# Head norms of a diffusion-transformer projection: the reciprocal root refined with one operand of every step in PSUM

## The chip, the core and the metric

The program runs on one core of one Trainium2 chip, as one launch. The metric is the device time of one execution in microseconds (us). The core has five engines that each work through their own queue in order: TensorE (PE in the profile; PEld is its loading of weights), VectorE (DVE), ScalarE (ACT), GpSimd (POOL) and SyncE (SP, which issues the DMAs here). They wait for one another through semaphores. On-chip data lies in SBUF, and in PSUM, into which TensorE writes its products.

## The reference, cut to what matters

Two layers of a hybrid backbone run over 128 context tokens and 1024 latent tokens of width 1024. Each layer projects the normalised tokens to a convolution input, to queries, keys and values of a grouped-query attention (GQA) and to those of a neighbourhood attention; after the mixing there is an output projection and an MLP. The change touches only the normalisation of the query and key heads, 64 wide:

```python
def _rms(x, g):
    xf = x.astype(jnp.float32)
    y = xf * lax.rsqrt(jnp.mean(xf * xf, axis=-1, keepdims=True) + EPS)
    return (y * g.astype(jnp.float32)).astype(x.dtype)
...
    qa = _rms(qa.reshape(B, L, GQA_HEADS, HEAD_DIM), aqg)
    ka = _rms(ka.reshape(B, L, GQA_KV_HEADS, HEAD_DIM), akg)
...
    qn = _rms(qn.reshape(B, L, NA_HEADS, HEAD_DIM), nqg)
    kn = _rms(kn.reshape(B, L, NA_HEADS, HEAD_DIM), nkg)
```

## The kernel before

Matrix products are done in float32 from split operands (high and low parts, three products each). The program is written out in a fixed order by nested Python generators; every engine executes its instructions in just that order, and the tile framework adds the semaphores. SBUF tiles come from tagged pools (T with 18 buffers, S with 18, U with 19, V with 24), PSUM tiles from one pool of eight banks (`P`, line 87): a new tile waits until the earlier user of its buffer is done.

The stage around the change is the projection (`project`, from line 689). Seven column blocks (A0 to A5 and VN, 256 columns each) are run over the nine token tiles in five groups, four of two tiles and one of a single tile. One such group does, in this order:

- `tok_group` (lines 534 to 544): 24 matmuls per token tile on TensorE into a PSUM bank `pst` (lines 541 to 543).
- In groups 1 and 3, `pr.step()`: the weights of the next column block are split, the high part `wh` on ScalarE (line 96) and the low part `wl` on VectorE (line 99), and further weights are requested.
- The first half of `post` (line 492): `head_stats` squares the heads on ScalarE (`sq`), sums them on VectorE (`ss`, line 420), and `rsq_start` takes Ln and Exp(-0.5 x) on ScalarE, which gives a first value `y` of the reciprocal root.
- A step of the convolution (`conv_taps`, line 572): the 31 taps of channel half 0 run on VectorE (`cacc<-cin,vecs,cacc`, 1167 wide), one or two in a step; 22 taps of half 1 run as a product on ScalarE (`cp`) and an addition on GpSimd (`cacc<-cacc,cp`, line 570).
- The second half of `post`: `head_norm` refines `y` by one Newton step, three scalar_tensor_tensor instructions on VectorE (`rsq_end`, lines 167 to 171, all recorded at line 102), each [128, 2 to 8] in size, and multiplies the heads by it (`xn<-pst,y`, line 99). GpSimd then applies gains (line 471) or rotary tables (lines 484 to 490) to `xn` and writes `o`.
- In groups 0, 2 and 4, a step of `fill`, the modulation for later in the layer (`modulation`, line 183): eight of its steps multiply into a bank `psmod` (line 224) with weights `aw` by DMA; then VectorE copies it (`mt<-psmod`, line 229), and at the next step TensorE transposes it (`psmt<-ident,mt`, line 233).
- `flush`: SyncE stores `o` of two groups before to DRAM (`ddA<-o`). From block A5 on the GQA's preparation (`kd<-ddA`, transposes at line 784) is interleaved.

`rsq_start` and `rsq_end` are shared with the row norms (lines 280, 282) and the convolution's layer norm (lines 744, 746), which the change leaves alone.

Of the kernel before, what the change touches and what calls it, by code (L numbers as in the profile page):

```python
# [14 lines left out]
ACTF = mybir.ActivationFunctionType  # L15
ALU = mybir.AluOpType
# [9 lines left out]
DH = 64  # L26
EPS = 1e-6
# [18 lines left out]
def hybrid_step(ctx, tc, I, O, depth=DEPTH):  # L46
# [7 lines left out]
    def nm(p):  # L54
        count[0] += 1
        return f"{p}{count[0]}"
# [4 lines left out]
    def T(shape, dt=F32, n="t"):  # L61
        return pers.tile([128] + list(shape), dt, tag="T", bufs=N_T, name=nm(n))
# [4 lines left out]
    def V(shape, n="v"):  # L67
        return pers.tile([128] + list(shape), F32, tag="V", bufs=24, name=nm(n))
# [18 lines left out]
    def P(n="ps"):  # L87
        return psum.tile([128, 512], F32, tag="p", bufs=8, name=nm(n))
# [3 lines left out]
    def act(out, in_, func, scale=1.0, bias=0.0, **k):  # L92
        nc.scalar.activation(out=out, in_=in_, func=func, scale=scale, bias=bias, **k)  # L93
# [4 lines left out]
    def tt(out, a, b, op, eng=None):  # L98
        (eng or nc.vector).tensor_tensor(out=out, in0=a, in1=b, op=op)  # L99

    def stt(out, a, s, b, op0, op1):
        nc.vector.scalar_tensor_tensor(out=out, in0=a, scalar=s, in1=b, op0=op0, op1=op1)  # L102
# [7 lines left out]
    eps = pers.tile([128, 1], F32, name="eps")  # L110
# [51 lines left out]
    def rsq_start(q, y, m):  # L162

        act(y, q, ACTF.Ln, scale=1.0 / m, bias=eps)
        act(y, y, ACTF.Exp, scale=-0.5)

    def rsq_end(q, y, t, m):

        stt(t, y, -0.5 / m, y, ALU.mult, ALU.mult)
        stt(t, q, EPS * m, t, ALU.add, ALU.mult)  # L170
        stt(y, t, 1.5, y, ALU.add, ALU.mult)
# [239 lines left out]
    def heads4(a, nt):  # L411

        return a.rearrange("p t (h d) -> p t h d", d=64)

    def head_stats(x, nt):
        n = nt * (x.shape[2] // 64)
        sq = T([nt, x.shape[2]], n="sq")
        act(sq, x, ACTF.Square)
        ss = V([n], "ss")
        nc.vector.tensor_reduce(out=ss, in_=sq.rearrange("p t (h d) -> p (t h) d", d=64), op=ALU.add, axis=AX.X)  # L420
        y = V([n], "y")
        rsq_start(ss, y, DH)
        return x, nt, n, ss, y

    def head_norm(x, nt, n, ss, y):
        rsq_end(ss, y, V([n], "nt"), DH)
        w = x.shape[2]
        xn = T([nt, w], n="xn")
        tt(heads4(xn, nt), heads4(x, nt), y.rearrange("p (t h) -> p t h", t=nt).unsqueeze(3).to_broadcast([128, nt, w // 64, 64]), ALU.mult)
        return xn  # L430
# [61 lines left out]
    def post(L, c, t, nt, ps):  # L492
# [5 lines left out]
        if normed is not None:  # L498
            st = head_stats(x[:, :, normed], nt)
# [4 lines left out]
        if normed is not None:  # L504
            xn = head_norm(*st)
            if c in ("A0", "A1"):
                post_rope(L, c, t, nt, xn, o)
            else:
                gain(o[:, :, normed], xn, 2 if c in ("A2", "A3") else 3, nt, L)
# [1473 lines left out]
```

## Time and profile before

| what | value |
|---|---|
| median of 3 runs | 2981.17 us (2978.42 to 2985.02) |
| the profiled execution | 2982.7 us, of which the span 2980.9 us |
| busy share of the span | PE 95%, PEld 85%, DVE 70%, ACT 47%, POOL 22% |
| mean granted TensorE clock | 0.983 of full |
| where the projections lie | about 100 to 350 us and 1590 to 1830 us |

The profile is one execution, recorded by the chip's profiler. Rows that group instructions name the line, the engine, the operation, the tiles written and read, the shapes and the count, then the busy time and the mean duration of one, and the engine's idle time before them with what ended it. An instruction's duration runs from its start on the engine to its end, so a wait inside the engine (for a memory port, say) lies in the duration, while a wait for a semaphore lies in the idle time before it. Many helpers record at one line (102 for every scalar_tensor_tensor), so groups are told apart by their tiles.

### The profile page before, as it was taken

To read this page: it belongs to the slowest core of one execution; us is meant where nothing else is said; L and a number is where in the kernel's file an instruction comes from. 1 tells how busy PE (TensorE), PEld (TensorE's weight loads), DVE (VectorE), ACT (ScalarE), POOL (GpSimd) and SP (SyncE) were. 2 spreads that over 40 slices of the span, in tenths; PEclk is the share of its full clock that TensorE was granted. 3 is DMA by queue.
4 is the path that set the end of the run, shared out by engine and by line. 5 is a ranking of instruction groups with operands and counts; after the bars stand their busy time and mean duration, and the time that the engine had idled before them with its cause. 6 is when DMAs were issued, how large, how long until landed. Compare 5 with 4: busy or idle time off the path is not lost.

```text
span 2980.9 us, 52857 instructions
## 1 busy us (share of the span) xinstructions
PE 2844.0 (95%) x20328; PEld 2525.2 (85%) x20328; DVE 2096.1 (70%) x4009; ACT 1401.0 (47%) x2864; POOL 652.5 (22%) x607
## 2 busy tenths in 40 slices
PE   6998999999999999999889989999999999999999
PEld 3878745789999989999868886458999999999999
DVE  6588778764867756768675877788557677585676
ACT  4333356762744443433452353668537444433343
POOL 3576345420000000000224772463100000000000
PEclk8999999999999999999999999999999999999999
DMA  7276302424466678443333672024245666565334
GB/s 286 85 210 167 106 20 61 102 65 139 148 212 198 208 239 300 161 156 96 122 129 106 187 200 75 16 55 111 89 124 179 207 203 196 201 236 183 116 102 161
DMA packets 434876, 444.05 MB, mean 149 GB/s; under 512 B 120512, under 2 KB 308672, under 8 KB 434624
## 3 DMA queue, kind: packets, MB, share of 16 engines
q1 hardware_dynamic: 434624, 440.67, 47.4%
q8 instruction: 160, 2.62, 0.4%
q14 instruction: 92, 0.75, 0.1%
HBM read 307.41 MB, written 133.17 MB: 148 GB/s over the span
## 4 chain that ended last, share of the span: by engine, by line
PE 76%; DVE 13%; ACT 4%; issue 2%; DMA 2%; POOL 2%; SPq 1%; DVEq 0%; POOLq 0%; ACTq 0%
PE ps L1319 23%; PE psb L1319 8%; PE psc L1319 6%; PE pso L1319 5%; PE psa L1319 5%; PE psd L1319 3%; PE psacc L1118 3%; PE pspv L985 2%; DVE cacc L102 2%; PE pspt L969 2%; PE pst L541 2%; PE pst L542 2%; PE pst L543 2%; PE psst L1132 2%; PE psm L1044 2%
## 5 line engine op out<-in xcount | busy, mean ns | idle before, releaser
L1319 PE MATMUL ps<-ts,w2h 128*128 128x288 f32 x3072 | 534.4, 296 | 8.3 <-DVE ts L99 4.8
L1319 PEld LDWEIGHTS ps<-ts,w2h 128*128 128x128 f32 x3072 | 451.7, 189 | 9.3 <-DVE ts L99 5.3
L1319 PE MATMUL ps<-ts,w2l 128*128 128x288 f32 x1536 | 329.2, 295 | 0.1
L96 ACT CAST ts<-ti 128x576 fp32r<-128x576 f32 x256 | 172.1, 672 | 310.2 <-PE ps L1319 208.6
L541 PE MATMUL pst<-wh,HA 128*128 128x256 f32 x1040 | 297.9, 286 | 0.0
L542 PE MATMUL pst<-wl,HA 128*128 128x256 f32 x1040 | 294.3, 283 | 0.2 <-DVE wl L99 0.2
L543 PE MATMUL pst<-wh,HA 128*128 128x256 f32 x1040 | 293.7, 282 | 0.0
L93 ACT ACTIVATE ev<-ev 128x576 f32<-128x576 f32 x240 | 164.7, 686 | 265.1 <-DVE ev L99 261.3
L1319 PEld LDWEIGHTS ps<-ts,w2l 128*128 128x128 f32 x1536 | 247.6, 189 | 0.4 <-DVE w2l L99 0.3
L102 DVE SCALAR_TENSOR_TENSOR X<-ps,mod,X 128x288 f32<-128x288 f32 x336 | 112.2, 410 | 163.5 <-PE ps L1319 163.5
L99 DVE TENSOR_TENSOR ts<-ti,ts 128x576 fp32r<-128x576 f32 x256 | 195.5, 764 | 44.7 <-ACT ts L96 44.7
L541 PEld LDWEIGHTS pst<-wh,HA 128*128 128x128 f32 x1040 | 198.3, 191 | 19.2 <-issue 6.9
L542 PEld LDWEIGHTS pst<-wl,HA 128*128 128x128 f32 x1040 | 198.2, 191 | 0.5 <-DVE wl L99 0.4
L543 PEld LDWEIGHTS pst<-wh,HA 128*128 128x128 f32 x1040 | 198.2, 191 | 0.0
L99 POOL TENSOR_TENSOR nacc<-nacc,nsq 128x512 f32<-128x512 f32 (+1 forms) x12 | 15.8, 1320 | 822.2 <-PE ps L1319 796.3
L1772 POOL COPY yu<-X 128x128 f32<-128x128 f32 x8 | 3.9, 500 | 836.2 <-DVE X L102 824.3
L1319 PE MATMUL pso<-HA,woh 128*128 128x288 f32 x1024 | 177.8, 295 | 0.0
L1046 DVE TENSOR_REDUCE mx<-psm 128x1 f32<-128x384 f32 x288 | 142.3, 547 | 30.1 <-PE psm L1044 30.0
L93 ACT ACTIVATE pt<-psst 128x512 f32<-128x512 f32 x216 | 118.1, 597 | 89.6 <-PE psst L1133 88.7
L99 POOL TENSOR_TENSOR R<-R,pt 128x1024 f32<-128x1024 f32 x60 | 148.3, 2472 | 26.3 <-ACT pt L93 24.3
L1319 PEld LDWEIGHTS pso<-HA,woh 128*128 128x128 f32 x1024 | 149.7, 188 | 0.0
L102 DVE SCALAR_TENSOR_TENSOR cacc<-cin,vecs,cacc 128x1167 f32<-128x1167 f32 x78 | 136.8, 1754 | 11.3 <-POOL cacc L570 10.1
(279 smaller groups left out, 7222.6 us busy)
## 6 DMA issues: line engine op xcount, KB each, us to landing
ti<-hd SPq DMA_DIRECT2D x128, 576.0 KB, 4.0
hd<-ev SPq DMA_DIRECT2D x224, 288.0 KB, 4.2
w1r<-in_mlp_w SPq DMA_DIRECT2D x176, 256.0 KB, 4.0
aw<-in_ada_w SPq DMA_DIRECT2D x160, 256.0 KB, 4.0
HF<-in_mlp_w SPq DMA_DIRECT2D x128, 256.0 KB, 5.3
ddA<-o SPq DMA_DIRECT2D x144, 128.0 KB, 3.0
wr<-in_w_in SPq DMA_DIRECT2D x28, 512.0 KB, 4.1
sd<-ev SPq DMA_DIRECT2D x24, 576.0 KB, 2.8
```

The source lines that it names most:

```text
L93: nc.scalar.activation(out=out, in_=in_, func=func, scale=scale, bias=bias, **k)
L96: nc.scalar.copy(out, in_)
L99: (eng or nc.vector).tensor_tensor(out=out, in0=a, in1=b, op=op)
L102: nc.vector.scalar_tensor_tensor(out=out, in0=a, scalar=s, in1=b, op0=op0, op1=op1)
L541: mm(o, hi, wh, start=(k == 0), stop=False)
L542: mm(o, hi, wl, start=False, stop=False)
L543: mm(o, lo, wh, start=False, stop=(k == KT - 1))
L969: nc.tensor.transpose(ps[0:n, c], self.p[j][:, o:o + n], ident)
L985: mm(ps[64 * j:64 * j + 64, 0:128], v[j], self.at[j, i], start=(i == 0), stop=(i == nb - 1))
L1046: nc.vector.tensor_reduce(out=mx[j][:, qt, b:b + 1], in_=ps[:, 0:384], op=ALU.max, axis=AX.X)
L1118: mm(acc[64 * j:64 * j + 64, :], v, pt[:, j, :], start=(kt == 0), stop=(kt == 8))
L1319: mm(ps[h][:, 0:HH], x, y[:, h * HH:(h + 1) * HH], start=(start and z == 0), stop=(stop and z == 2), skip_group_check=True)
```

## The change

`head_stats` no longer calls `rsq_start`. It takes a PSUM bank `pss`, in which two small areas z and t lie, and ScalarE writes the first value twice: once as z in PSUM, once as y in SBUF. `head_norm` does the same Newton step as before, y * (1.5 - 0.5 * (ss/64 + eps) * y * y), with z and t in PSUM: in each of the three instructions one tensor operand is in PSUM and the other in SBUF, where before both were in SBUF. The number of VectorE instructions stays; ScalarE has one Exp more in each of the 60 head norms, and 60 more tiles are taken from the eight PSUM banks.

```diff
         y = V([n], "y")
-        rsq_start(ss, y, DH)
-        return x, nt, n, ss, y
-
-    def head_norm(x, nt, n, ss, y):
-        rsq_end(ss, y, V([n], "nt"), DH)
+        small = P("pss")
+        z, t = small[:, 0:n], small[:, 64:64 + n]
+        act(y, ss, ACTF.Ln, scale=1.0 / DH, bias=eps)
+        act(z, y, ACTF.Exp, scale=-0.5)
+        act(y, y, ACTF.Exp, scale=-0.5)
+        return x, nt, n, ss, y, z, t
+
+    def head_norm(x, nt, n, ss, y, z, t):
+
+        stt(t, y, -0.5 / DH, z, ALU.mult, ALU.mult)
+        stt(z, ss, EPS * DH, t, ALU.add, ALU.mult)
+        stt(y, z, 1.5, y, ALU.add, ALU.mult)
         w = x.shape[2]
```

## The prediction

> **What bounds the kernel now.** I read the page first, then the busy times by stretch, then TensorE's waits in the two stretches where head norms run, and last the order of instructions around the longest of these waits.
>
> ```profile
> span 2980.9 us, 52857 instructions
> PE 2844.0 (95%) x20328; PEld 2525.2 (85%) x20328; DVE 2096.1 (70%) x4009; ACT 1401.0 (47%) x2864; POOL 652.5 (22%) x607
> ```
> ```profile
> 100.00:350.00 250.00, 233.01 (x1798) 207.42 (x1797) 182.36 (x249) 84.87 (x171) 148.46 (x118) 0.97 0.59 163
> 190.00:257.00 67.00, 61.28 (x500) 58.12 (x499) 60.18 (x66) 22.94 (x44) 42.02 (x21) 0.95 0.62 163
> ```
>
> In the second fence the columns after the length are the busy time of PE, PEld, DVE, ACT and POOL, then the granted TensorE clock. TensorE sets the time: in the projection of the first layer it is busy 233 of 250 us, so a change to VectorE can only win what lies in the 17 us where TensorE stands, plus what the stops do to its clock. VectorE is at its limit only locally: 60.2 of 67 us between 190 and 257.
>
> TensorE's own waits in the first layer's stretch, and the matching one of the second layer (us in total, times, longest):
>
> ```profile
> PE psmod L224 <- DMA aw<-in_ada_w: 5.9, 5, 1.7
> PE psmt L233 <- DVE mt L229: 5.7, 1, 5.7
> PE pstr L784 <- DMA kd<-ddA: 3.1, 1, 3.1
> ```
> ```profile
> PE psmt L233 <- DVE mt L229: 5.5, 1, 5.5
> PE pstr L784 <- DMA kd<-ddA: 2.4, 1, 2.4
> ```
>
> The one that VectorE causes is `mt`, the copy of the modulation's product: 5.7 + 5.5 = 11.2 us. The copy itself is short; it comes late because VectorE's queue is late:
>
> ```profile
> 241.43 0.69 DVE L99 TENSOR_TENSOR xn<-pst,y 128x512 f32<-128x512 f32 x1
> 242.04 0.68 DVE L229 COPY mt<-psmod 128x512 f32<-128x512 f32 x1
> ```
> ```profile
> 242.87 1.09 PE L233 MATMUL psmt<-ident,mt 128*128 128x128 f32 x4 [5.72 <-DVE mt L229]
> ...
> 244.40 0.41 PE L541 MATMUL pst<-wh,HA 128*128 128x256 f32 x1
> 244.61 0.41 PE L542 MATMUL pst<-wl,HA 128*128 128x256 f32 x1
> ...
> 247.60 0.28 PE L543 MATMUL pst<-wh,HA 128*128 128x256 f32 x1
> 247.72 0.28 PE L541 MATMUL pst<-wh,HA 128*128 128x256 f32 x1
> ```
>
> TensorE had nothing from 237.15 (242.87 less 5.72). After the stop its matmuls start every 0.21 us, three us later every 0.12: the stop also costs clock.
>
> **The change part by part.** The three steps of the root write and read [128, 2 to 8]. Over both layers, minimum, median and maximum in ns, with the multiplication behind them for comparison:
>
> ```profile
> L102 DVE SCALAR_TENSOR_TENSOR nt<-y x60: 147/223/2679, 120.4 to 1785.5; 128x8 f32<-128x8 f32 x32, 128x4 f32<-128x4 f32 x24, 128x2 f32<-128x2 f32 x4
> L102 DVE SCALAR_TENSOR_TENSOR y<-nt,y x60: 161/168/2645, 120.8 to 1787.4; 128x8 f32<-128x8 f32 x32, 128x4 f32<-128x4 f32 x24, 128x2 f32<-128x2 f32 x4
> L99 DVE TENSOR_TENSOR xn<-pst,y x60: 291/691/693, 121.0 to 1790.2; 128x512 f32<-128x512 f32 x32, 128x256 f32<-128x256 f32 x24, 128x128 f32<-128x128 f32 x4
> ```
> ```profile
> 194.95 2.89 DVE L102 SCALAR_TENSOR_TENSOR cacc<-cin,vecs,cacc 128x1167 f32<-128x1167 f32 x2
> 197.76 2.66 DVE L102 SCALAR_TENSOR_TENSOR nt<-y 128x4 f32<-128x4 f32 x1
> 200.45 0.16 DVE L102 SCALAR_TENSOR_TENSOR nt<-ss,nt 128x4 f32<-128x4 f32 x1
> ```
> ```profile
> 197.18 3.22 POOL L570 TENSOR_TENSOR cacc<-cacc,cp 128x1167 f32<-128x1167 f32 x1 [3.49 <-ACT cp L93]
> ...
> 203.85 2.71 POOL L570 TENSOR_TENSOR cacc<-cacc,cp 128x1167 f32<-128x1167 f32 x1 [1.66 <-ACT cp L93]
> ```
>
> A step with four elements per partition takes 2.66 us when GpSimd's addition runs (197.18 + 3.22 = 200.40; the step ends at 200.42), and 0.16 us otherwise. So a VectorE instruction with two SBUF inputs stands until GpSimd's instruction is over. `xn`, with one input in PSUM, sits right behind the steps and in 60 cases never exceeds 0.693 us. That is the evidence that the new form does not stand. What the steps cost in all:
>
> ```profile
> L102 DVE SCALAR_TENSOR_TENSOR nt<-y 128x8 f32<-128x8 f32 (+2 forms) x60 | 41.7, 696 | 13.3 <-ACT y L93 13.3
> L102 DVE SCALAR_TENSOR_TENSOR y<-nt,y 128x8 f32<-128x8 f32 (+2 forms) x60 | 32.1, 535 | 2.1
> L102 DVE SCALAR_TENSOR_TENSOR nt<-ss,nt 128x8 f32<-128x8 f32 (+2 forms) x60 | 22.1, 368 | 2.1
> ```
>
> 41.7 + 32.1 + 22.1 = 95.9 us for 180 steps; at 0.165 us each, about their undisturbed duration, they need 29.7. So 66 us of standing goes, 33 in each layer. Most is off the path: where VectorE keeps up with TensorE it then only waits longer for the next squares.
>
> How much of the 5.7 us stop goes depends on the queue between 190 and 257, where VectorE's backlog forms. Removed standing can come back in VectorE's other instructions with two SBUF inputs, the taps and `wl`, because they share the same port with GpSimd. I therefore add up what the port must carry there:
>
> ```profile
> L570 POOL TENSOR_TENSOR cacc<-cacc,cp 128x1167 f32<-128x1167 f32 x10 | 30.2, 3019 | 16.2 <-ACT cp L93 16.2
> L471 POOL TENSOR_TENSOR o<-xn,gains 128x512 f32<-128x512 f32 x4 | 7.2, 1801 | 5.0 <-DVE xn L99 5.0
> L471 POOL TENSOR_TENSOR o<-xn,gains 128x256 f32<-128x256 f32 x5 | 4.7, 933 | 3.2 <-DVE xn L99 3.2
> ```
> ```profile
> L102 DVE SCALAR_TENSOR_TENSOR cacc<-cin,vecs,cacc 128x1167 f32<-128x1167 f32 x14 | 26.8, 1916 | 0.2
> L102 DVE SCALAR_TENSOR_TENSOR nt<-y 128x4 f32<-128x4 f32 x4 | 8.1, 2031 | 0.0
> L99 DVE TENSOR_TENSOR wl<-wr,wh 128x1024 fp32r<-128x1024 f32 x3 | 6.1, 2033 | 0.2 <-ACT wh L96 0.2
> ```
>
> GpSimd: 10 x 2.71 = 27.1 us of additions, and at most 7.2 + 4.7 = 11.9 of gains. VectorE: 14 taps at 2.89/2 = 1.45, 20.2 us; three `wl`, an estimate of 1.3 each from the tap's time and their 1024 to 1167 elements, 3.8. Together 63.0 of 67 us; the 27 steps add 27 x 0.165 = 4.5 and fill the stretch entirely (67.5). So the port is full before, and the change takes about 4.5 us of its load away, and with it the pairs of instructions that waited on each other. As the gains' rows still hold GpSimd's own standing, 11.9 is an upper end and the slack rather 6 to 7 us. I take 5 us less backlog at `mt` in each layer. That leaves a stop of 0.7 and 0.5 us, and a gain of 10 us over both layers.
>
> The clock in a stretch with short stops of TensorE (at most 1.7 us each, the `psmod` row), and behind the two stops for `mt`:
>
> ```profile
> 145.00:150.00 5.00, 2.17 (x9) 0.47 (x7) 4.71 (x7) 0.60 (x1) 4.92 (x6) 1.00 0.90 264
> ```
> ```profile
> 243.00:246.00 3.00, 3.00 (x15) 3.00 (x16) 3.00 (x3) 0.78 (x3) 0.47 (x1) 0.50 0.53 112
> 1723.00:1727.00 4.00, 4.00 (x28) 4.00 (x27) 3.84 (x8) 1.94 (x4) 0.67 (x1) 0.75 0.61 131
> ```
>
> Half a clock over 3 us is 1.5 us, a quarter less over 4 us is 1.0. Short stops leave the clock at 1.00 (2.17 of 5 us busy in the first row), so residues under 1 us should too: 2.5 us gained. [...]
>
> What the change adds:
>
> ```profile
> L99 DVE TENSOR_TENSOR mod<-psmt,vecs x12: 157/165/175, 44.8 to 1835.4; 128x16 f32<-128x16 f32 x12
> L93 ACT ACTIVATE y<-y x60: 203/208/211, 117.5 to 1785.2; 128x8 f32<-128x8 f32 x32, 128x4 f32<-128x4 f32 x24, 128x2 f32<-128x2 f32 x4
> L102 DVE SCALAR_TENSOR_TENSOR nt<-psn,nt x14: 224/691/692, 40.9 to 2248.0; 128x512 f32<-128x512 f32 x8, 128x64 f32<-128x64 f32 x4, 128x128 f32<-128x128 f32 x2
> ```
>
> A small VectorE instruction with an input in PSUM takes 0.165 us, as the steps do now: 0 for the new operand. The other end is the 0.224 us of a step with PSUM at 64 wide, 0.06 more: 27 x 0.06 = 1.6 us of backlog. Writing to PSUM has no small row; I let these ends hold it too, and take 0 since the read's row is nearest in size. [...]
>
> The extra Exp is 60 x 0.21 = 12.6 us on ScalarE, which is busy 85 of 250 us. It is covered, except that `cp` and GpSimd's addition queue behind it: nine groups by 0.2 is 1.8 us of GpSimd's 16.2 us of waiting in the stretch, which is one reason to take 5 us and not 6. Without any cover, the 13.3 us that VectorE waits for `y` would grow by a third, 4.4 us.
>
> `aw` (5.9 us) waits in SyncE's queue, whose transfers need buffers that GpSimd's rotary products release. GpSimd loses the port to three steps per group, about 0.5 us; five groups lie ahead: 0 to 2.5 us per layer. I take 0.5 per layer, 1 in all. `kd` stands behind the store of an `o` that is late by the same backlog; TensorE arrives some 6 us earlier, and the store too. I take 0; ends are the whole wait gained (5.5 us) and all of the gain given back.
>
> Sum: 10 + 2.5 + 1 = 13.5 us. From the profiled execution's 2982.7 us (span 2980.9, 1.8 around it) that gives 2969.2. That execution lies 1.5 us above the median of the runs, so the median comes to about 2968 us.
>
> **The rivals.**
> - More goes (0.18). TensorE's `kd` waits vanish as well (5.5 us), and `aw` gives 5 in place of 1: another 9.5, 2958 us. For it: both hang on GpSimd's `o`. Against: they end with transfers, not with VectorE.
> - The port stays the bound (0.11). The taps take up the standing that the steps lose, as the sum of 63.0 of 67 allows if GpSimd's gaps cannot be used. Then perhaps 1.5 us per layer and no clock is won: 2978.
> - The next wait absorbs it (0.08). TensorE comes 6 us sooner to `kd`, whose transfer does not move, and the stops of 3.1 and 2.4 us grow by as much: only `aw`'s 1 us and half of the clock's 2.5 are left, 2979.
> - Slower through PSUM (0.05). A bank per head norm makes each group take two of eight banks. A group's 48 matmuls at 0.118 us are 5.7 us, and TensorE may now run ahead by three to four groups, 17 to 22 us, if banks are reused in turn; the last step of a group ended as late as
>
> ```profile
> 256.12 0.16 DVE L102 SCALAR_TENSOR_TENSOR y<-nt,y 128x4 f32<-128x4 f32 x1
> ```
>
>   19.1 us after TensorE had finished that group at 237.15. With the backlog cut by 5 us this does not bite. If the order of reuse allows a lead of only one group, TensorE loses up to 19.1 - 5.7 - 5.7 (the stop it already has) = 8 us per layer: 2997. It decides from the point where the lead is shorter than the backlog.
> - No effect (0.03): the new operands stand for the port all the same, 2981. `xn`'s 693 ns maximum speaks against it.
>
> [...]
>
> **How the numbers follow.** The forecast has 0.55. Its own range, with the residue of the stops between 0 and 2.5 us per layer and 0 to 5 us for `aw`, is 2962 to 2974. A difference of 0.2%, 6 us, is about what a measurement of this kernel tells from none; faster means below 2975.2. Faster: 0.55 + 0.18, and two thirds of the 0.11 for the port, if it loses only half: 0.80. Within: the rest of that case, the absorbed one and no effect, 0.15. Slower: 0.05. The range leaves out half of the slow end and of the best case's tail: 2956 to 2979.
>
> **What would show it.** Right: the three steps at 0.16 to 0.2 us at most, 180 of them under 35 us; taps and `wl` longer by some us in sum; `psmt` waiting for `mt` under 1.5 us in each projection; the granted clock 1.00 behind it. `kd` and `aw` about as before. Wrong: steps with durations over 1 us; `pst` waiting for a VectorE instruction at the start of a group (banks); `kd` stops of 6 us and more; or a `psmt` wait still above 4 us with taps that grew by 10 us or more.

## The result and the profile after

| | before | after |
|---|---|---|
| median (5 runs each on one chip) | 2981.17 us (2978.42 to 2988.66) | 2960.81 us (2955.55 to 2969.27) |
| the profiled execution | 2982.7 us | 2955.6 us |

The ratio is 0.9928, 95% interval 0.9905 to 0.9951: 20.4 us less. Forecast were 13.5 us less and 2968 us, with a range of 2956 to 2979. A second measurement of the unaltered changed kernel on another chip (the run e11 below) gave 2960.28 us, ratio 0.9921 (0.9905 to 0.9938).

First the page's head of the kernel after, then the groups of the three steps, of the taps and of `wl` (busy us, mean ns of one, idle time before them):

```profile
span 2953.8 us, 52917 instructions
PE 2840.5 (96%) x20328; PEld 2520.6 (85%) x20328; DVE 2036.7 (69%) x4009; ACT 1413.2 (48%) x2924; POOL 658.6 (22%) x607
```
```profile
L102 DVE SCALAR_TENSOR_TENSOR cacc<-cin,vecs,cacc 128x1167 f32<-128x1167 f32 x78 | 132.4, 1697 | 18.5 <-POOL cacc L577 17.3
L99 DVE TENSOR_TENSOR wl<-wr,wh 128x1024 fp32r<-128x1024 f32 x33 | 61.5, 1863 | 31.7 <-ACT wh L96 26.3 <-issue 4.6 <-POOL o L478 0.8
...
L102 DVE SCALAR_TENSOR_TENSOR pss<-ss,pss 128x8 f32<-128x8 f32 (+2 forms) x60 | 10.1, 168 | 2.1
L102 DVE SCALAR_TENSOR_TENSOR y<-pss,y 128x8 f32<-128x8 f32 (+2 forms) x60 | 9.8, 164 | 2.0
L102 DVE SCALAR_TENSOR_TENSOR pss<-y,pss 128x8 f32<-128x8 f32 (+2 forms) x60 | 9.7, 162 | 17.9 <-ACT y L93 17.9
```

The 180 steps take 10.1 + 9.8 + 9.7 = 29.6 us instead of 95.9, and none stands any more.

Where the time went is read from stretches with the same work. The first layer's begin at 100 us and end as the attention's first scores behind the projection start; the second layer's begin and end with its projection. The matmul counts agree within a few. The first fence is before, the second after. The columns after the length are the busy time of PE, PEld, DVE, ACT and POOL, then the granted clock, DMA share and GB/s.

```profile
100.00:349.00 249.00, 232.01 (x1795) 206.67 (x1794) 182.36 (x249) 83.96 (x170) 148.46 (x118) 0.97 0.60 163
1586.00:1818.00 232.00, 219.04 (x1738) 196.06 (x1741) 178.41 (x240) 80.98 (x165) 149.29 (x118) 0.99 0.61 167
```
```profile
100.00:336.00 236.00, 228.30 (x1796) 202.86 (x1795) 152.03 (x249) 90.42 (x200) 151.75 (x118) 0.99 0.63 174
1569.00:1792.00 223.00, 216.79 (x1740) 193.80 (x1738) 150.26 (x239) 87.57 (x195) 151.50 (x118) 1.00 0.64 174
```

The first layer's stretch is 13 us shorter and the second's 9: 22 us in the two projections, all that the medians show. A second execution of the changed kernel (e11 below) took 12.6 us longer in all, yet the same two stretches are 13.8 and 9.1 us shorter in it than before. The length less PE's busy time is TensorE's standing. It falls from 17.0 to 7.7 and from 13.0 to 6.2 us, 16.0 us together. The other 6.0 us are busy time: the same matmuls take 232.01 - 228.30 and 219.04 - 216.79 us less, and the granted clock goes from 0.97 to 0.99 and from 0.99 to 1.00, as it is no longer lowered behind the two stops at `mt` and the first layer's at `kd` (the rows stand in the section on why the prediction was right). VectorE is busy 30 and 28 us less and TensorE wins less than that: most of the 66 us was beside the path, as forecast.

The profiled executions differ by 27 us. Part of the other 5 us changes from one execution to the next: the wait of `psmu` for the last tap was 3.18 us in the first layer before, and in two executions of the same changed kernel (after, then e11) it is

```profile
345.15 1.13 PE L736 MATMUL psmu<-cacc,ones 128*128 128x512 f32 x2 [0.81 <-DVE cacc L102]
```
```profile
347.57 1.12 PE L736 MATMUL psmu<-cacc,ones 128*128 128x512 f32 x2 [3.07 <-DVE cacc L102]
```

TensorE's waits in the two stretches (us in total, times, longest): the first layer after, then a row of the second layer before that the prediction did not show, then the second layer after:

```profile
PE psmod L224 <- DMA aw<-in_ada_w: 5.0, 5, 1.4
...
PE pstr L791 <- ACT sq L93: 0.4, 1, 0.4
```
```profile
PE psmod L224 <- DMA aw<-in_ada_w: 4.8, 4, 1.7
```
```profile
PE psmod L224 <- DMA aw<-in_ada_w: 4.5, 5, 1.4
PE pstr L791 <- ACT y L93: 1.7, 1, 1.7
```

`mt`, 5.7 and 5.5 us before, is no longer listed. Its copy and TensorE's transposes of it, in the first layer after:

```profile
233.48 0.68 DVE L229 COPY mt<-psmod 128x512 f32<-128x512 f32 x1
```
```profile
235.88 0.60 PE L233 MATMUL psmt<-ident,mt 128*128 128x128 f32 x4
```

The copy ended 5.6 us behind TensorE's arrival before (242.04 + 0.68 against 237.15) and ends 1.7 us ahead of it now. `kd`, 3.1 and 2.4 before, has turned into waits of the same transposes for something else, 0.4 and 1.7. `aw` is nearly as before.

### The profile page after: what moved, and what is told of

Its sections match the earlier page's. It is cut to its first block, busy times and chain, and to the rows that moved or that the text cites. A ratio compares the mean times of both kernels' runs of the same rounds, so it can differ in the third digit from the quotient of the medians.

```text
span 2953.8 us, 52917 instructions
## 1 busy us (share of the span) xinstructions
PE 2840.5 (96%) x20328; PEld 2520.6 (85%) x20328; DVE 2036.7 (69%) x4009; ACT 1413.2 (48%) x2924; POOL 658.6 (22%) x607
## 4 chain that ended last, share of the span: by engine, by line
PE 82%; DVE 9%; ACT 3%; DMA 2%; issue 2%; POOL 2%; SPq 0%; DVEq 0%; POOLq 0%; ACTq 0%
PE ps L1326 24%; PE psb L1326 7%; PE psc L1326 6%; PE pso L1326 5%; PE psa L1326 5%; PE pst L548 4%; PE pst L549 3%; PE pst L550 3%; PE psd L1326 3%; PE psacc L1125 3%; PE pspv L992 2%; PE pspt L976 2%; PE psst L1139 2%; PE psmod L224 2%; PE psm L1051 2%
## 5 line engine op out<-in xcount | busy, mean ns | idle before, releaser
L102 DVE SCALAR_TENSOR_TENSOR cacc<-cin,vecs,cacc 128x1167 f32<-128x1167 f32 x78 | 132.4, 1697 | 18.5 <-POOL cacc L577 17.3
```

## The experiments

The theory: an instruction of VectorE with two inputs in SBUF stands while GpSimd works on SBUF (one step took 2.66 us and ended with GpSimd's addition, where the next took 0.16); one operand in PSUM spares it that (none of the 60 `xn` took over 0.693 us); what TensorE gains is VectorE's backlog in the blocks A2 and A3. The rivals are told with each run. Each ratio is against executions of the kernel before taken beside the run on the same chip, with medians of 2979.6 to 2984.4 us.

### Is it the operand, or something beside it?

**e1_bank_only** takes the bank and the extra Exp, and leaves the steps in SBUF:

```diff
-        stt(t, y, -0.5 / DH, z, ALU.mult, ALU.mult)
-        stt(z, ss, EPS * DH, t, ALU.add, ALU.mult)
-        stt(y, z, 1.5, y, ALU.add, ALU.mult)
+        rsq_end(ss, y, V([n], "nt"), DH)
```

> The bank is taken and ScalarE writes the first value into it as well (the extra Exp), but the three steps read and write SBUF as before; the copy in PSUM is read by nobody. Theory (the steps stand while GpSimd reads SBUF, and an operand in PSUM spares them that): no gain, 2981 us, at most 3 us more for the extra Exp; the 180 steps take 90 to 100 us in sum, TensorE's two stops for mt together 11 us or more. Rival (the gain comes from beside the steps: another order of the PSUM banks, or a shift on ScalarE): 2961 to 2971 us with steps still at 90 to 100 us.

Measured: 2982.01 us, ratio 0.9995 (0.9984 to 1.0006). The steps take 43.3 + 27.9 + 16.6 = 87.8 us, a little under what was expected, and the stops at `mt` come to 8.0 us where 11 were expected. No gain without the operand. The run also holds a lesson on `mt`: TensorE's waits, by layer,

```profile
PE psmod L224 <- DMA aw<-in_ada_w: 6.3, 6, 1.7
PE psmt L233 <- DVE mt L229: 4.0, 1, 4.0
PE pstr L789 <- DMA kd<-ddA: 2.6, 1, 2.6
```
```profile
PE psmod L224 <- DMA aw<-in_ada_w: 5.0, 5, 1.3
PE psmt L233 <- DVE mt L229: 4.0, 1, 4.0
PE pstr L789 <- DMA kd<-ddA: 3.6, 1, 3.6
PE pst L547 <- DVE wl L99: 0.9, 1, 0.9
```

show 3.2 us less at `mt`, but `kd`, `wl` and `aw` are 2 us longer in sum, and the time is that of before. A shorter stop is not yet time.

**e8_no_pool_adds** is the kernel before without GpSimd's 42 additions:

```diff
-                nc.gpsimd.tensor_tensor(out=acc[:, 0:CW], in0=acc[:, 0:CW], in1=p, op=ALU.add)
+                pass
```

> The kernel before, without GpSimd's additions of the convolution's products (the taps of half 1 that ScalarE multiplies are computed and not added); steps in SBUF as before. Theory (what a step stands for is GpSimd's use of the same port): with 42 additions of 2.7 us gone, the 180 steps fall from 95.9 us to 30 to 45 us without any operand in PSUM (the rest stands for GpSimd's gains and rotary products), and the time to the changed kernel's 2961 us or below. Rival (the steps stand for something else, DMA traffic or ScalarE): the 180 steps stay above 70 us.

```profile
L102 DVE SCALAR_TENSOR_TENSOR nt<-y 128x8 f32<-128x8 f32 (+2 forms) x60 | 14.9, 249 | 13.3 <-ACT y L93 13.3
...
L102 DVE SCALAR_TENSOR_TENSOR y<-nt,y 128x8 f32<-128x8 f32 (+2 forms) x60 | 12.3, 205 | 2.0
L102 DVE SCALAR_TENSOR_TENSOR nt<-ss,nt 128x8 f32<-128x8 f32 (+2 forms) x60 | 11.8, 197 | 2.1
```

39.0 us with all operands in SBUF, where the kernel before has 95.9, and 2957.84 us, ratio 0.9914 (0.9895 to 0.9934), from two executions only. What the steps stand for is mostly GpSimd's addition: 56.9 of the 66 us go with it. The time says less than the steps do: this kernel computes something else, 42 additions of 2.7 us are gone from GpSimd's queue, and taps and `wl` are 10.0 and 8.4 us shorter as well, so how much of the gain comes from the steps was not shown.

**e2_first_only** puts one operand of the first step into PSUM and leaves the other two steps in SBUF:

```diff
+        t = V([n], "nt")
         stt(t, y, -0.5 / DH, z, ALU.mult, ALU.mult)
-        stt(z, ss, EPS * DH, t, ALU.add, ALU.mult)
-        stt(y, z, 1.5, y, ALU.add, ALU.mult)
+        stt(t, ss, EPS * DH, t, ALU.add, ALU.mult)
+        stt(y, t, 1.5, y, ALU.add, ALU.mult)
```

> Only the first of the three steps has an operand in PSUM; it writes its result to SBUF, and steps two and three have both inputs in SBUF as before. Theory: the standing belongs to whichever two-SBUF instruction comes next while GpSimd's instruction runs, so it moves from the first step to the second and third: first step 0.16 us throughout, the 180 steps together still 70 to 95 us, mt stops together 7 to 11 us, time 2973 to 2981 us. Rival (each step stands on its own account, and 32 of the 66 us of standing sit in the first): the 180 steps together near 63 us, half of the gain, 2971 us, with the second and third step at their former 22 and 32 us.

```profile
L102 DVE SCALAR_TENSOR_TENSOR cacc<-cin,vecs,cacc 128x1167 f32<-128x1167 f32 x78 | 142.4, 1826 | 16.1 <-POOL cacc L578 14.9
L99 DVE TENSOR_TENSOR wl<-wr,wh 128x1024 fp32r<-128x1024 f32 x33 | 57.6, 1745 | 27.4 <-ACT wh L96 22.4 <-issue 4.6
...
L102 DVE SCALAR_TENSOR_TENSOR nt<-ss,nt 128x8 f32<-128x8 f32 (+2 forms) x60 | 39.9, 665 | 2.1
L102 DVE SCALAR_TENSOR_TENSOR y<-nt,y 128x8 f32<-128x8 f32 (+2 forms) x60 | 17.0, 284 | 2.1
L102 DVE SCALAR_TENSOR_TENSOR nt<-y,pss 128x8 f32<-128x8 f32 (+2 forms) x60 | 9.2, 153 | 17.9 <-ACT y L93 17.9
```

2976.66 us, ratio 0.9983 (0.9972 to 0.9994). Neither expectation fits whole. The second step takes 39.9 us instead of 22.1, as the theory has it: it stands in the first one's place. The third takes 17.0 instead of 32.1, which nobody expected, so the sum, 66.1 us, lies near the rival's 63. But the time moves by some 5 us, not 10. Taps and `wl`, 5.6 and 4.3 us longer, do not explain that: in e11, with all three steps freed, they are 2.3 and 8.4 us longer and the gain is whole. What fits is where the steps still stand. Between 186 and 258 us, ahead of and around `mt`, the three took 20.3 us before and take 16.8 here, 13.4 of it in the second, against 5.9 in the changed kernel; the stops at `mt` are still 3.2 and 3.1 us.

### Where the gain comes from

**e3_A2_A3** and **e4_not_A2_A3** split the change by column block: with `c` handed to `head_stats`, either only A2 and A3 or only the other four get the new form (e4 has the opposite condition).

```diff
+        if c not in ("A2", "A3"):
+            rsq_start(ss, y, DH)
+            return x, nt, n, ss, y, None, None
         small = P("pss")
...
+        if z is None:
+            rsq_end(ss, y, V([n], "nt"), DH)
```

> Steps with an operand in PSUM for the column blocks A2 and A3 alone, which run from 186 to 257 us ahead of and around the mt copy; A0, A1, A4 and A5 as before. Theory (the backlog ahead of mt forms in these two blocks): the mt stops go from 11.2 to under 2 us and the slow clock behind them too, about 13 us, 2968 us; the stops for kd stay near 5.5 us in sum unless they hang on this backlog as well, in which case 2963 us. Rival (backlog carried over from the earlier blocks A0 and A1): mt stops still 5 us or more together, 2973 us or more.

> The complement: an operand in PSUM for the blocks A0, A1, A4 and A5, and both operands in SBUF for A2 and A3. Theory: mt stops as before, 10 us or more together; what is gained lies behind them, kd (5.5 us and the slow clock of some 2.5 us behind one of its stops) and the wait of psmu for cacc (2.4 us of 3.2): at best 2973 us, at least 2981 us. If kd and psmu keep their stops here, they too hang on the backlog of A2 and A3, and the time is 2980 us. Rival (the gain lies in the count of steps, wherever they run): two thirds of the gain, 2967 us.

e3: 2959.88 us, ratio 0.9922 (0.9909 to 0.9935), a larger gain than either figure of the theory, 2968 or 2963 us. e4: 2982.54 us, ratio 1.0000 (0.9991 to 1.0010). The whole gain sits in A2 and A3. TensorE's waits in the first layer, e3 and then e4:

```profile
PE psmod L224 <- DMA aw<-in_ada_w: 5.9, 6, 1.7
...
PE pstr L797 <- DMA kd<-ddA: 1.4, 1, 1.4
```
```profile
PE psmt L233 <- DVE mt L229: 5.8, 1, 5.8
...
PE pstr L797 <- DMA kd<-ddA: 2.8, 1, 2.8
```

In e3 the steps of the other four blocks still take 23.6 + 16.1 + 14.2 = 53.9 us, of which 34 are standing (120 steps at 0.165 us need 19.8): that costs no time that shows. In e4 the 60 steps of A2 and A3 take 23.4 + 8.5 + 8.2 = 40.1 us, 30 of them standing: these cost everything. And `kd`, whose stop comes in A5, shrinks when A2 and A3 are changed and stays when A4 and A5 are. So it hangs on the same backlog.

How it does is seen on the queues, before and then after: GpSimd's `o` that is the last ahead of `kd` in SyncE's queue (before, with ScalarE's wait for VectorE ahead of it), SyncE's issues, TensorE's transposes of `kd`.

```profile
274.96 0.30 ACT L93 ACTIVATE y<-ss,eps 128x8 f32<-128x8 f32 x1 [4.92 <-DVE ss L420]
```
```profile
279.48 1.28 POOL L471 TENSOR_TENSOR o<-xn,gains 128x512 f32<-128x512 f32 x1
```
```profile
281.16 2.68 SPq L144 DMA_DIRECT2D ddA<-o  x4
283.94 0.63 SPq L144 DMA_DIRECT2D kd<-ddA  x1
```
```profile
288.85 1.09 PE L784 MATMUL pstr<-ident,kd 128*128 128x128 f32 x4 [3.08 <-DMA kd<-ddA]
```
```profile
268.36 1.29 POOL L478 TENSOR_TENSOR o<-xn,gains 128x512 f32<-128x512 f32 x1
```
```profile
269.68 2.09 SPq L144 DMA_DIRECT2D ddA<-o  x4
271.81 1.07 SPq L144 DMA_DIRECT2D kd<-ddA  x1
```
```profile
277.37 0.63 PE L791 MATMUL pstr<-ident,kd 128*128 128x128 f32 x4 [0.44 <-ACT sq L93]
```

The load of `kd` stands in SyncE's queue behind the store of an `o`, and `o` behind VectorE, by way of ScalarE: `o` starts as GpSimd's addition ends (276.81 to 279.52 us), and ScalarE made that addition's product only after it had waited 4.92 us for VectorE's sum `ss`; in the kernel after that wait is 2.60 us. `o` is 11.1 us earlier, the load 12.1, and TensorE (start less wait: 285.77 and 276.93) only 8.8. The difference of 3.3 us is more than the stop of 3.08.

**e6_mt_later** leaves the backlog of the kernel before and moves TensorE's question:

```diff
             nc.vector.tensor_copy(mt, ps)
             yield
+            if not first:
+                yield
             pt = P("psmt")
```

> The kernel before, steps in SBUF as they were, with one more step of the generator between the copy mt and TensorE's transposes of it, so that TensorE asks for mt one or two groups (6 to 12 us) later. Theory (what costs is VectorE's backlog in A2 and A3, and mt is only where TensorE meets it first): the mt stops vanish, but the stops behind them grow, kd from 5.5 us to 8 us or more in sum and wl or squares join in; time 2975 to 2981 us. Rival (the stop at mt is the whole cost, the rest has slack): 11.2 us and the slow clock of 2.5 us go, 2968 us, kd as before.

2986.94 us, ratio 1.0010 (1.0001 to 1.0019): a trifle slower, where the theory had 2975 to 2981. TensorE's waits, first and second layer:

```profile
PE psmod L224 <- DVE psmod L219: 10.0, 1, 10.0
```
```profile
PE pst L544 <- DVE wl L99: 6.3, 1, 6.3
...
PE psmod L224 <- DVE psmod L219: 2.2, 1, 2.2
```

The stop at `mt` is gone, and other waits for VectorE stand in its place, though not at `kd`, where the theory had put them. The second layer shows it cleanly, 6.3 us at `wl`. In the first, part of the 10.0 us comes from the edit itself, since the clearing of the next `psmod` now lies one group ahead of its first matmul; three steps queued ahead of it stand as well (0.90, 1.19 and 2.57 us in the timeline). The rival, 2968 us, is out.

### What is left of the steps, and of standing elsewhere

**e5_no_steps** leaves the refinement out, and with it the extra Exp and the bank:

> The changed kernel without the Newton refinement: the three steps and the extra Exp are left out, and the heads are multiplied by the first value of the root, so this computes a coarser root. Theory (after the change what is left of the steps, 29.6 us on VectorE, lies beside TensorE's work and holds nobody up): within 3 us of the changed kernel, 2958 to 2961 us, mt and kd stops under 2 us each. Rival (VectorE still limits the blocks A2 and A3, and its last 4 to 5 us of steps there count): 2950 to 2955 us.

2952.56 us, ratio 0.9899 (0.9885 to 0.9913). The theory said nothing would come, the rival 2950 to 2955. Against the changed kernel's second measurement, 0.9921 (0.9905 to 0.9938), it is about 7 us, with intervals that overlap a little; TensorE's waits for `aw` are 3.0 and 3.5 us, where they were 5.0 and 4.5. Even steps that do not stand probably still cost a few us; that it is the steps and not the Exp was not tested apart, but e1 took the Exp and the bank at no cost that shows.

**e7_ln_too** gives the same form to the root of the convolution's layer norm, which lies behind the projection:

```diff
-            rsq_start(pv[:, 0:n], y, 256)
+            z = P("psz")[:, 0:n]
+            act(y, pv[:, 0:n], ACTF.Ln, scale=1.0 / 256, bias=eps)
+            act(z, y, ACTF.Exp, scale=-0.5)
+            act(y, y, ACTF.Exp, scale=-0.5)
             yield
-            rsq_end(pv[:, 0:n], y, sqs[1], 256)
+            stt(sqs[1], y, -0.5 / 256, z, ALU.mult, ALU.mult)
+            stt(z, pv[:, 0:n], EPS * 256, sqs[1], ALU.add, ALU.mult)
+            stt(z, z, 1.5, y, ALU.add, ALU.mult)
...
-                tt(a, a, y, ALU.mult)
+                tt(a, a, z, ALU.mult)
```

> The changed kernel, with the same treatment for the root of the convolution's layer norm (six roots, 128 to 512 wide): z in a PSUM bank, each of the three steps and the product with the root with one operand in PSUM, one Exp more on ScalarE for each. Theory (standing costs only where TensorE waits for VectorE's queue; behind the projection TensorE waits 2.3 to 2.5 us at nmx and 0.8 us at psmu and psvr): the steps' standing goes, but at most 2 us of time, 2958 to 2961 us. Rival (the rest of TensorE's stops there come from this standing as well): 2953 to 2956 us. If the six longer Exps delay ScalarE: up to 2963 us.

2944.93 us, ratio 0.9867 (0.9851 to 0.9883), far more than the 2 us of the theory and more than the rival's. Repeated, unaltered:

> The kernel with the layer norm's root in the new form as well, once more, unaltered: it ran at 0.987 of the kernel before, and the one with two more instructions in the new form at 0.990. If the second loses by its longer hold on the bank, this comes to 0.985 to 0.988 again, 2941 to 2947 us; if the two differ by the chance of a run alone, it comes to 0.989 to 0.991, 2950 to 2956 us.

e12: 2944.07 us, ratio 0.9878 (0.9854 to 0.9902). So this version beats both kernels. The same stretch of the first layer's attention, TensorE's waits and the stretch's row, in the changed kernel and then in e7:

```profile
PE psst L1139 <- DVE mx L1053: 2.8, 1, 2.8
PE psnm L1042 <- DVE nmx L1036: 2.5, 1, 2.5
...
350.00:430.00 80.00, 72.65 (x299) 37.09 (x296) 63.02 (x105) 42.37 (x82) 38.64 (x20) 0.94 0.06 19
```
```profile
PE psst L1144 <- ACT pt L93: 0.7, 1, 0.7
PE psnm L1047 <- DVE nmx L1041: 0.6, 1, 0.6
...
350.00:422.00 72.00, 69.30 (x309) 35.77 (x309) 57.84 (x106) 44.33 (x87) 37.19 (x19) 1.00 0.07 21
```

With ten matmuls more, the stretch is 8 us shorter in one layer, and the medians of the two kernels differ by 16. Two stops of 2.5 and 2.8 us shrink to 0.6 and 0.7, and the clock rises from 0.94 to 1.00. I had priced the stops alone, and again not the clock behind them.

**e9_ln_all** puts two more instructions of that norm into the new form, in the same bank (a square, and the sigmoid):

```diff
-                sq = T([n], n="lsq")
+                sq = T([n], n="lsq") if j else z
...
-                sigmoid_end(sg)
+                act(sg, sg, ACTF.Exp)
+                act(sg, sg, ACTF.Ln, bias=ones[:, 0:1])
+                act(z, sg, ACTF.Exp, scale=-1.0)
                 yield
-                tt(a, a, sg, ALU.mult)
+                tt(a, a, z, ALU.mult)
```

> As in the run before with the root of the layer norm, and two more of its instructions get one operand in PSUM, in the same bank: the sum of the two squares (one square is written to PSUM) and the product with the sigmoid. Theory, corrected by that run (behind the projection too VectorE's queue is late where TensorE waits for nmx and mx, so standing taken out ahead of these waits is time): the sum of squares, 2.9 us instead of 0.7 ahead of TensorE's last psvr wait of 0.3 us, and the product, 1.7 instead of 0.7, lie between waits that are already short; 0 to 3 us more than that run, 2942 to 2945 us. Rival (every us of standing removed there is a us of time, three blocks of each layer): 2936 us or less. Other rival (the bank is held longer, and TensorE or ScalarE waits for it): 2948 us or more.

2953.06 us, ratio 0.9898 (0.9882 to 0.9913): no further gain, and by its median 8 to 9 us above e7 and e12, though its interval overlaps that of e12. Its profile has a wait of 1.3 us for `nmx` in each layer (at 490 us in the first) that e7 and e12 do not have. Whether the longer hold on the bank is the cause was not shown.

**e10_ln_all_A2_A3** is e9 with the condition of e3:

> The same layer norm, and operands in PSUM in the head norms of the blocks A2 and A3 alone, so 40 Exps and 40 banks fewer and some 34 us of standing more, all of it in A0, A1, A4 and A5. Theory (that standing is beside TensorE's work): within 2 us of the kernel with all head norms. Rival (with TensorE further ahead, the standing in A4 and A5 begins to count): 4 us or more above it.

2952.12 us, ratio 0.9884 (0.9864 to 0.9905), as e9: the standing in the other blocks is still beside the work.

**e11_after_again** is the changed kernel as it stands, told above:

> The changed kernel once more, unaltered, to have its time beside the others on the same chip: 2961 us, 0.992 to 0.994 of the kernel before. If it comes to 0.990 or below, leaving out the refinement (2952.6 us) gained nothing beside it; at 0.9925 that run's 3 us or more stand as a gain from VectorE's last steps.

## Why the prediction was right, and where it was short

The sign and the mechanism held; the size was 13.5 us, where 20.4 were measured. Step by step:

- **The steps.** Forecast 0.165 us each and 66 us of standing gone: 0.162 to 0.168 and 66.3. The price of the operand in PSUM, taken at 0, is 0 within a few ns: the shortest of each step is 147, 161 and 161 ns before and 151, 165 and 159 after.
- **Most of it beside the path.** Right, and e3 shows which part: 34 us of standing in A0, A1, A4 and A5 cost nothing that shows.
- **`mt`, 10 us taken.** 11.2 us before, not listed after. "I take 5 us less backlog at `mt` in each layer" was low by 2 us: against TensorE's arrival the copy came 7.3 us earlier in the first layer and 7.0 in the second. That the term was off by only 1.2 us in sum is luck, as no more than the stops of 5.7 and 5.5 us could be won there. e3 and e4 show that the gain came from the stretch that was costed.
- **The clock, 2.5 us taken.** 6.0 us measured. I looked behind the stops at `mt` alone, and not far enough there. A row of the kernel before, just behind the window that was priced, and then 8 us behind the first layer's stop at `kd`, before and after:

```profile
246.00:247.00 1.00, 1.00 (x7) 1.00 (x7) 0.91 (x4) 1.00 (x2) 0.04 (x1) 0.50 0.86 187
288.00:296.00 8.00, 7.15 (x38) 7.18 (x39) 3.46 (x6) 4.19 (x7) 6.08 (x4) 0.57 1.04 287
```
```profile
276.00:284.00 8.00, 7.56 (x64) 6.96 (x67) 2.48 (x6) 4.99 (x10) 5.14 (x4) 1.00 1.03 283
```

  The first slow stretch thus lasts from 242.87 to about 247 us, 4.1 us, and the second layer's from 1722.17 to about 1725, 2.8 us: at half clock an estimate of 2.1 and 1.4 us lost, where 1.5 and 1.0 were taken. Behind `kd` it is 38 matmuls in 8 us against 64, at half clock until about 294.6 us, an estimate of 2.9 us. The three make 6.4, near the 6.0. The rows of the kernel before were there to be read ahead of the change.
- **`kd`, 0 taken.** This is the step that failed. It said "TensorE arrives some 6 us earlier, and the store too". TensorE came 8.8 us earlier and the load 12.1, because the load hangs on the end of the whole chain (VectorE, ScalarE, GpSimd, SyncE) that had been late, and TensorE's arrival only on its own stops. 5.5 us of `kd` became 0.4 + 1.7: 3.4 us gained. The rival "more goes" had this part, together with 5 us of `aw` that did not come.
- **`aw`, 1 us taken.** 5.9 + 4.8 before, 5.0 + 4.5 after: 1.2.
- **The extra Exp, taken as covered.** For VectorE it is not: it waits 17.9 us for `y` where it was 13.3, 4.6 us more and so about the 4.4 named as the end without cover. But TensorE does not notice: e3 with 40 Exps fewer is not faster.
- **Taps and `wl` longer.** Right in sum: 190.1 us before, 193.9 after and 200.8 in e11. The growth is in `wl`, from 53.3 to 61.5 and 61.7; the taps, 136.8 before, took 132.4 and 139.1 in two executions of the changed kernel.

The sum as measured: 11.2 at `mt`, 3.4 at `kd`, 1.2 at `aw`, 6.0 of clock, 21.8 us of the 22 in the two stretches. The forecast case's own range, 2962 to 2974, missed 2960.8 by 1.2 us, since `kd` and its clock were not in it; the wider one held it. Of the rivals, "the port stays the bound" and "the next wait absorbs it" are out by the changed kernel's own waits: none for `mt`, and 0.4 and 1.7 us where `kd` stood. "Slower through PSUM" is out too: no `pst` waits for VectorE at a group's start.

## What to carry to other kernels

Price a backlog at all the waits that hang on it, not at the one where it shows first. Moving the first wait (e6) won nothing, and removing 30 us of standing ahead of it (e3) won its stop, part of the next one and the clock behind both. For every stop of TensorE that may go, read the granted clock in the few us behind it. Small VectorE instructions with two SBUF inputs deserve a look wherever GpSimd runs: one operand in PSUM took them out of its way here, 180 steps in 29.6 us instead of 95.9, and it paid only ahead of a wait of TensorE.

## What the runs showed of the hardware

- A step of [128, 2 to 8] with one operand in PSUM takes 0.161, 0.170 and 0.166 us at the median (first, second and third), about what the second and third took at the median with both in SBUF, 0.167 and 0.168. ScalarE's small Exp is even shorter into PSUM, 0.180 us at the median, than into SBUF before the change (0.208).
- Standing moves in part to the next instruction with two SBUF inputs, and in part goes: with the first of three steps freed (e2), the second took 17.8 us more, out of 32.5 us taken off the first, and the third 15.1 less.
- What the prediction calls a port that VectorE shares with GpSimd is the author's reading of times. A step with both inputs in SBUF that began under GpSimd's addition took 2.66 us and ended with it, at 200.42 and 200.40 us; that addition, begun under a tap of VectorE, took 3.22 us, where the next took 2.71. Without the additions (e8) steps, taps and `wl` are 56.9, 10.0 and 8.4 us shorter. What in the core makes them stand was not shown.
- Behind the stop of 3.08 us at `kd` in the first layer the granted clock was 0.50, from 288 us until about 294.6; behind the 2.42 us at `kd` in the second layer it stayed at 1.00. The length alone does not tell the two apart: in the kernel after, behind the 2.48 us at `nmx` (the matmuls go on at 367.13 us), it was 0.50 from 368 to 374 us.
